# V of both mixers with tokens stationary and 512 weight columns moving, in rows of tokens

## The chip, the cores and the metric

One core of one Trainium2 chip runs the whole program. The metric is the device time of one execution in microseconds (us). The kernel before took 1684.07 us (median of 3 runs, 1683.81 to 1688.92). TensorE (PE) multiplies: a stationary operand of up to 128 columns is loaded into it (the profile's PEld rows), then a moving operand streams past it and the result lands in PSUM, in banks of 128 x 512 fp32. VectorE (DVE), ScalarE (ACT) and GpSimd (POOL) do the elementwise work, and the DMA queue of SyncE (SP) moves nearly all data, issuing in order.

## What is computed

One layer of a streaming encoder, for 1024 new tokens of a prompt and 32 tokens of a running stream that has a cache of 512: 1056 tokens, width 1024, fp32. Cut to what matters here:

```
h = rmsnorm(x, g_mix)
z = h @ w_in                       # q,k,v of mixer A (512 columns each), indexer, q,k,v of mixer B, gates
v_a = z[..., 1024:1536]            # 8 heads of 64
score = sum_h relu(q_i . k_i) * w_i ; idx = top_k(score, 256)      # which keys mixer A may see
o_a = softmax(q_a . k_a / 8 over idx) @ v_a
o_b = stick_breaking(q_b . k_b / 8) @ v_b
h2 = x + w_out(sigmoid(g_a) * (o_a @ w_ba) + sigmoid(g_b) * (o_b @ w_bb))
y = h2 + w_down(relu(w_up rmsnorm(h2))^2)
```

v_a and v_b are outputs too, with shape (tokens, 8, 64). The change touches how v_a and v_b are made, and nothing else of the mathematics.

## The kernel before

**Numbers.** Every fp32 operand x is split into a high part (`xh`, a copy rounded to the fast matmul type) and a rest (`xl`); a product takes three matmuls: high by high, rest by high, high by rest. A unit of weights is 128 x 512: a DMA into `wst`, a cast by ACT into `wh`, a subtraction on POOL into `wl`. Five places (`WB`) hold such pairs, and three buffers hold raw units. The first norm's factor per token is applied to the projection after the matmul: `rs` holds it per token in a column, `rb` spread along tokens in a row.

**Stages.** (1) index projection, to about 80 us; (2) q, k, v of mixer B for four pairs of heads, with the indexer's scores between them; (3) the top-k, a search by bits on DVE and ACT (tile `junk`, 31 bits in two groups of token tiles), then the masks; (4) two gates, and for each pair of heads of mixer A: V, then q and k (tile `qk`); (5) more gates, attention B, attention A, with gates and branch products as filler; (6) from about 915 us the merge and the feed-forward part.

**V before** (`project_v(p, mixer, w, vout)`, called at the end of `project_b` and the start of `project_a`, four times each). The weights are stationary, 128 columns of one pair of heads, and tokens move: chunks of 512, 272 and 272, eight steps of k, three matmuls each, so 72 matmuls per call, into the banks `pj` (two of them). DVE multiplies each chunk by `rb` into `vt` (head columns on partitions, tokens along), which is stored as the transposed output. The attention needs V with tokens on partitions, so PE transposes `vt` in 9 blocks of 128 into bank `t`, ACT copies the high half of each head into `vs`, DVE makes the rest, and a DMA stores `vs` to `dv`.

**What sets the order.** All work is recorded as nodes of a plan (`Plan`), and each engine's order is written out by it ahead of the run, from its own costs: among the nodes whose inputs are there, the one of the lowest rank number, then the oldest. Ranks are `FAST` (evictions), `PREP` (weights), `MAIN`, `FILL` (column-block matmuls) and `SLOW` (the top-k). On the chip each queue then runs strictly in that order and waits where the plan was wrong.

Of the kernel before, what the change touches and what calls it, by code (L numbers as in the profile page):

```python
# [10 lines left out]
F32 = mybir.dt.float32  # L11
F32R = mybir.dt.float32r
# [3 lines left out]
AF = mybir.ActivationFunctionType  # L16
# [40 lines left out]
FAST, PREP, MAIN, FILL, SLOW = 0, 1, 2, 3, 4  # L57


def rows(s):  # L60

    return DEC if s == NEW else 128
# [7 lines left out]
GROUPS = (range(0, 4), range(4, 8), range(8, 9))  # L70
# [391 lines left out]
class Layer:  # L462
# [103 lines left out]
    def run(self):  # L566
        nc, a = self.nc, self.a
# [11 lines left out]
        c = lambda shape, dt, name: nc.tile(self.const, shape, dt, name)  # L579
# [66 lines left out]
        for p in range(2, 4):  # L646
            self.project_b(p)
            with nc.behind():
                old, new = a["ck" + "ba"[p - 2]], self.dc[H * (3 - p):H * (4 - p)]
                nc.sync.dma_start(*(z.rearrange("j e t -> (j e) t") for z in (new, old)))  # L650
        with nc.rank(SLOW):
            self.top_k_begin()
        gates = iter([*range(KB, 2 * KB), *range(KB)])
        for _ in range(2):
            self.gate(next(gates), "zb")
        self.early(*(a["w_va"][0, j] for j in range(2)), *(a["w_qka"][0, j] for j in range(3)))
        nc.close(self.pr, self.ik)
        self.pr = nc.open("proja")
        self.rope_tables()
        for p in range(4):  # L660
            self.project_a(p)
        with nc.rank(SLOW):
# [390 lines left out]
                self.ts_[:, :, j].rearrange("p t (s e) -> p t s e", s=2),  # L1053
                S.rearrange("p t (s e) -> p t s e", s=2), gx)

    def project_v(self, p, mixer, w, vout):

        nc, pr = self.nc, self.pr
        units = [self.unit(w[p, j]) for j in range(2)]
        vt = nc.tile(pr, [128, T], F32, "vt", bufs=1)  # L1060

        def done(c, cs, ps):
            nc.vector.tensor_mul(vt[:, cs], ps, self.rb[:, cs])

        self.column_block(units, self.x_of, done, self.parts)
        nc.sync.dma_start(vout[p * 128:p * 128 + 128], vt)
        for sl in GROUPS:
            pt = self.bank("t")
            m = rows(sl[0])
            nt = len(sl)  # L1070
            for i, s in enumerate(sl):
                nc.tensor.transpose(pt[:m, i * 128:i * 128 + 128], vt[:, 128 * s:128 * s + m], self.ident)
            vs = nc.tile(pr, [128, 2, 4, 128], F32R, "vs", bufs=1)
            pv = pt.rearrange("p (t h e) -> p h t e", t=4, h=2)
            for h in range(2):
                vh = vs[:m, h, :nt, 0:HD]
                nc.scalar.copy(vh, pv[:m, h, :nt])
                nc.vector.tensor_sub(vs[:m, h, :nt, HD:], pv[:m, h, :nt], vh.bitcast(F32))
            for h in range(2):
                nc.sync.dma_start(self.dv[mixer * H + 2 * p + h, :m, sl[0]:sl[0] + nt], vs.bitcast(F32)[:m, h, :nt])  # L1080

    def keep(self, dst, g, cs, z):

# [4 lines left out]
    def project_b(self, p):  # L1088
        nc, pr, a = self.nc, self.pr, self.a
        for name, dst in (("w_qb", self.dq), ("w_kb", self.dk)):  # L1090
            units = [self.unit(a[name][p, j]) for j in range(2)]

            def done(c, cs, ps, name=name, dst=dst):
                n = cs.stop - cs.start
                z = nc.tile(pr, [128, 512], F32, "zb", bufs=2)[:, :n]
                zz = nc.tile(pr, [128, 2, 512], F32R, "zz", bufs=2)[:, :, :n]
                nc.vector.tensor_mul(z, ps, self.rb[:, cs])
                nc.scalar.copy(zz[:, 0], z)
                nc.gpsimd.tensor_sub(zz[:, 1], z, zz.bitcast(F32)[:, 0])
                if name == "w_kb":  # L1100
                    nc.sync.dma_start(self.o["k_b"][p * 128:p * 128 + 128, cs], z)
                self.keep(dst, H + 2 * p, cs, zz)

            self.column_block(units, self.x_of, done, self.parts)
        self.project_v(p, 1, a["w_vb"], self.o["v_b"])

    def project_a(self, p):
        nc, pr, a = self.nc, self.pr, self.a
        self.project_v(p, 0, a["w_va"], self.o["v_a"])
        units = [self.unit(a["w_qka"][p, j]) for j in range(4)]  # L1110
        qk = nc.tile(pr, [128, NT, 4, HD], F32, "qk", bufs=1)
        ss = nc.tile(pr, [128, NT, 4], F32, "ss", bufs=2)
# [2 lines left out]
        for s in range(NT):  # L1115
            m = rows(s)
# [687 lines left out]
def _host_arrays(inp):  # L1804
    f = {k: np.asarray(v) for k, v in inp.items()}

    def units(w):
        k, m = w.shape
        return np.ascontiguousarray(
            w.reshape(k // 512, 4, 128, m // 128, 128).transpose(3, 0, 2, 1, 4).reshape(m // 128, k // 512, 128, 512))  # L1810
# [10 lines left out]
        np.concatenate([qi[:, :256], ki, wi], axis=1).reshape(KB, 128, NI_A).transpose(1, 0, 2).reshape(128, KB * NI_A))  # L1821
    out["w_ib"] = np.ascontiguousarray(
        qi[:, 256:].reshape(4, 2, 128, NI_B).transpose(0, 2, 1, 3).reshape(4, 128, 512))
    out["w_qb"], out["w_kb"], out["w_vb"], out["w_va"] = units(qb), units(kb), units(vb), units(va)
# [26 lines left out]
    return out  # L1851


_OUTS = {"yT": (128, KB, T), "k_a": (T, 512), "v_a": (512, T), "k_idx": (T, HD), "k_b": (512, T), "v_b": (512, T)}


def _build(nc, arrays):
# [29 lines left out]
```

## Time and profile before

| | |
|---|---|
| median of 3 runs | 1684.07 us |
| span of the profiled execution, first to last instruction | 1682.7 us |
| what lies around the span, by the median | 1.4 us |
| PE busy / PEld busy | 1662.1 us (99%) / 1585.9 us (94%) |
| DVE / ACT / POOL busy | 1368.9 us (81%) / 947.7 us (56%) / 799.9 us (48%) |
| granted TensorE clock | 1.000 throughout |
| DMA, mean | 173 GB/s |
| first and last transposition of V | 119.5 us, 428.4 us |

The profiled execution has no time of its own beside its span here; the span with 1.4 us stands for the median run. Of a matmul the profile gives a start and a modelled end: a 272-column matmul is shown as 0.29 us long although the next one starts about 0.13 us after it. What a matmul costs a busy TensorE is therefore read from start to start, not from its length. Everything recorded through the plan has the line of the plan's own call, so groups are told apart by tile names.

### The profile page before, as it was taken

To read this page: it belongs to the slowest core of one execution; us is meant where nothing else is said; L and a number is where in the kernel's file an instruction comes from. 1 tells how busy PE (TensorE), PEld (TensorE's weight loads), DVE (VectorE), ACT (ScalarE), POOL (GpSimd) and SP (SyncE) were. 2 spreads that over 40 slices of the span, in tenths; PEclk is the share of its full clock that TensorE was granted. 3 is DMA by queue.
4 is the path that set the end of the run, shared out by engine and by line. 5 is a ranking of instruction groups with operands and counts; after the bars stand their busy time and mean duration, and the time that the engine had idled before them with its cause. 6 is when DMAs were issued, how large, how long until landed. Compare 5 with 4: busy or idle time off the path is not lost.

```text
span 1682.7 us, 34767 instructions
## 1 busy us (share of the span) xinstructions
PE 1662.1 (99%) x12226; PEld 1585.9 (94%) x12226; DVE 1368.9 (81%) x2875; ACT 947.7 (56%) x2024; POOL 799.9 (48%) x682
## 2 busy tenths in 40 slices
PE   7999999999999999999999999999999999999999
PEld 7998999999989999998999999999999999999999
DVE  8777899997569898887877649998988998679775
ACT  6556788765366767896665546333333454443431
POOL 5423332344346566354556437543433466345563
PEclk9999999999999999999999999999999999999999
DMA  7234454354583636688774643444443597676674
GB/s 260 83 103 116 139 182 144 110 150 142 161 230 97 189 88 190 173 262 256 214 204 132 186 128 127 140 151 151 151 143 135 181 327 237 203 220 210 222 227 136
DMA packets 180685, 290.29 MB, mean 173 GB/s; under 512 B 29312, under 2 KB 60512, under 8 KB 180480
## 3 DMA queue, kind: packets, MB, share of 16 engines
q1 hardware_dynamic: 180224, 287.75, 55.2%
q8 instruction: 96, 1.57, 0.4%
q14 instruction: 77, 0.63, 0.1%
q10 hardware_dynamic: 288, 0.34, 0.1%
HBM read 195.09 MB, written 94.90 MB: 172 GB/s over the span
## 4 chain that ended last, share of the span: by engine, by line
PE 87%; DVE 6%; DMA 3%; issue 2%; POOL 1%; ACT 1%; SPq 0%; DVEq 0%; ACTq 0%; POOLq 0%
PE pj L442 35%; PE c L442 11%; PE a L442 11%; PE b L442 11%; PE s L442 10%; PE o L442 5%; PE t L442 5%; DVE junk L442 2%; DMA wst<-w_ba 1%; POOL wl L442 1%; DVE y L442 0%; DMA vc<-cva 0%; DVE small L442 0%; DMA wst<-w_ib 0%; DMA xl<-du 0%
## 5 line engine op out<-in xcount | busy, mean ns | idle before, releaser
L442 PE MATMUL pj<-xl,wh 128*128 128x272 f32 (+2 forms) x1200 | 333.9, 312 | 0.0
L442 POOL TENSOR_TENSOR wl<-wst,wh 128x512 fp32r<-128x512 f32 x125 | 175.8, 1411 | 215.2 <-ACT wh L442 201.8
L442 PE MATMUL pj<-xh,wh 128*128 128x272 f32 (+1 forms) x768 | 251.8, 328 | 0.0
L442 PE MATMUL pj<-xh,wl 128*128 128x272 f32 (+1 forms) x768 | 250.6, 327 | 0.2 <-POOL wl L442 0.2
L442 PEld LDWEIGHTS pj<-xl,wh 128*128 128x128 f32 x1200 | 212.7, 188 | 9.9
L442 ACT CAST wh<-wst 128x512 fp32r<-128x512 f32 x197 | 120.5, 619 | 128.1 <-PE pj L442 34.6
L442 PEld LDWEIGHTS pj<-xh,wl 128*128 128x128 f32 x768 | 144.6, 188 | 10.6 <-POOL wl L442 0.5
L442 PEld LDWEIGHTS pj<-xh,wh 128*128 128x128 f32 x768 | 144.7, 188 | 10.2 <-DVE gz L442 0.3
L442 POOL TENSOR_TENSOR p<-p,rem 128x383 f32<-128x383 f32 (+8 forms) x66 | 104.8, 1603 | 66.4 <-DVE rem L442 29.1
L442 ACT CAST wh<-us 128x512 fp32r<-128x512 f32 x80 | 49.7, 621 | 115.9 <-PE pj L442 29.3
L442 DVE TENSOR_TENSOR tt<-t,tt 128x512 fp32r<-128x512 f32 (+2 forms) x168 | 100.2, 620 | 16.4 <-ACT tt L442 15.7
L442 DVE TENSOR_TENSOR_SCAN rem<-rem,first 128x384 f32<-128x384 f32 (+8 forms) x66 | 108.9, 1668 | 2.0 <-ACT rem L442 1.6
L442 POOL TENSOR_TENSOR wl<-y,wh 128x512 fp32r<-128x512 f32 x46 | 68.5, 1491 | 77.8 <-ACT wh L442 73.0
L442 ACT ACTIVATE junk<-score,cand 128x1024 bf16<-128x1024 f32 (+2 forms) x93 | 96.9, 1042 | 12.0 <-DVE cand L442 10.4
L442 ACT CAST wh<-y 128x512 fp32r<-128x512 f32 x79 | 48.9, 621 | 96.1 <-PE c L442 20.7
L442 ACT CAST tt<-t 128x512 fp32r<-128x512 f32 (+2 forms) x168 | 85.8, 540 | 27.3 <-PE t L442 18.3
L442 PE MATMUL o<-tt,v 128*128 128x256 f32 (+1 forms) x640 | 98.7, 279 | 1.2 <-DVE o L442 0.6
L442 PE MATMUL s<-k,q 128*128 128x512 f32 (+4 forms) x384 | 98.3, 352 | 0.6 <-issue 0.6
L442 PEld LDWEIGHTS o<-tt,v 128*128 128x128 f32 x640 | 90.5, 189 | 7.4 <-ACT tt L442 1.4
L442 DVE TENSOR_SCALAR_CACHE_REDUCE junk<-score,cand 128x384 bf16<-128x384 f32 (+1 forms) x124 | 92.9, 749 | 3.1
L442 PE MATMUL t<-ident,p 128*128 128x128 f32 (+1 forms) x596 | 90.8, 275 | 0.0
L442 POOL TENSOR_SCALAR p<-p,nb 128x384 f32<-128x384 f32 (+6 forms) x66 | 53.5, 817 | 70.6 <-DVE nb L442 57.8
(380 smaller groups left out, 5646.3 us busy)
## 6 DMA issues: line engine op xcount, KB each, us to landing
us<-w_down SPq DMA_DIRECT2D x80, 256.0 KB, 3.5
q<-dq SPq DMA_DIRECT2D x64, 256.0 KB, 4.3
du<-us SPq DMA_DIRECT2D x56, 264.0 KB, 2.7
du<-y SPq DMA_DIRECT2D x56, 264.0 KB, 3.1
y<-w_up SPq DMA_DIRECT2D x44, 256.0 KB, 2.8
k<-dk SPq DMA_DIRECT2D x40, 256.0 KB, 4.5
v<-dv SPq DMA_DIRECT2D x40, 256.0 KB, 4.2
xl<-du SPq DMA_DIRECT2D x35, 264.0 KB, 5.2
```

The costliest lines, as they stand in the source:

```text
L442: fn(*args, **kw)
```

## The change

`project_v` now makes all 512 columns of one mixer in one call. The tokens are stationary (`xh`, `xl` of one token tile) and the 512 weight columns move. Four token tiles at once fill four banks (`V_BANKS`: `pj`, `s`, `pj`, `s`), then five tiles (the last has the 32 new tokens, 64 stationary columns, two matmuls a step, and a joining addition) fill `pj`, `s`, `pj`, `s`, `s`. Each group of tiles walks the eight units of weights, so each unit is loaded twice. A finished bank is scaled by `rs` on ACT into `vz` (two buffers), which is stored as the output in rows of tokens; ACT casts the high half into `vs` (two buffers of 128 x 8 x 128) and DVE or POOL makes the rest; one DMA per tile stores all eight heads to `dv`. No transposition of V is left. V of mixer B comes after all four q and k of mixer B, V of mixer A before the first q and k of mixer A. The weights and outputs have a new layout, and the scratch that is set aside for software-driven DMA is cut to 1024.

```diff
+V_BANKS = ('pj', 's', 'pj', 's', 's')
...
+        self.project_v(1, a["w_vb"], self.o["v_b"])
         with nc.rank(SLOW):
             self.top_k_begin()
...
-        self.early(*(a["w_va"][0, j] for j in range(2)), *(a["w_qka"][0, j] for j in range(3)))
+        self.early(*(a["w_va"][k] for k in range(WB)))
...
+        self.project_v(0, a["w_va"], self.o["v_a"])
         for p in range(4):
             self.project_a(p)
...
-    def project_v(self, p, mixer, w, vout):
-        units = [self.unit(w[p, j]) for j in range(2)]
-        vt = nc.tile(pr, [128, T], F32, "vt", bufs=1)
-        def done(c, cs, ps):
-            nc.vector.tensor_mul(vt[:, cs], ps, self.rb[:, cs])
-        self.column_block(units, self.x_of, done, self.parts)
-        nc.sync.dma_start(vout[p * 128:p * 128 + 128], vt)
-        for sl in GROUPS:
-            pt = self.bank("t")
...
-                nc.tensor.transpose(pt[:m, i * 128:i * 128 + 128], vt[:, 128 * s:128 * s + m], self.ident)
-            vs = nc.tile(pr, [128, 2, 4, 128], F32R, "vs", bufs=1)
...
+    def project_v(self, mixer, w, vout):
+        mm = nc.tensor.matmul
+        for tiles in (range(0, 4), range(4, NT)):
+            banks = [self.bank(V_BANKS[i]) for i in range(len(tiles))]
+            for k in range(KB):
+                wh, wl = self.unit(w[k])
+                with nc.rank(FILL):
+                    for s, ps in zip(tiles, banks):
+                        first, last = k == 0, k == KB - 1
+                        if s == NEW:
+                            x = self.xh[1][:, k, SEQ - W1:]
+                            mm(ps[:2 * DEC], x, wh, start=first, stop=False)
+                            mm(ps[:2 * DEC], x, wl, start=False, stop=last)
+                            continue
+                        xh, xl = self.x_of(k, slice(128 * s, 128 * s + 128))
+                        mm(ps, xh, wh, start=first, stop=False)
+                        mm(ps, xh, wl, start=False, stop=False)
+                        mm(ps, xl, wh, start=False, stop=last)
+            for s, ps in zip(tiles, banks):
+                m = rows(s)
+                with nc.rank(FAST):
+                    if s == NEW:
+                        self.join(ps, nc.tile(pr, [128, 512], F32, "vz", bufs=2)[:DEC])
+                    z = nc.tile(pr, [128, 512], F32, "vz", bufs=2)
+                    nc.scalar.activation(z[:m], ps[:m], AF.Copy, scale=self.rs[:m, s:s + 1])
+                    vs = nc.tile(pr, [128, H, 128], F32R, "vs", bufs=2)
+                    zv = z.rearrange("p (h e) -> p h e", h=H)
+                    nc.scalar.copy(vs[:m, :, 0:HD], zv[:m])
+                nc.either.tensor_sub(vs[:m, :, HD:], zv[:m], vs.bitcast(F32)[:m, :, 0:HD])
+                nc.sync.dma_start(vout[128 * s:128 * s + m], z[:m])
+                nc.sync.dma_start(
+                    self.dv[mixer * H:mixer * H + H, :m, s].rearrange("g p e -> p g e"), vs.bitcast(F32)[:m])
...
-        self.project_v(p, 1, a["w_vb"], self.o["v_b"])
...
-        self.project_v(p, 0, a["w_va"], self.o["v_a"])
```

**PE, V of mixer B.** Before, in the third pair of heads (rows read "bank <- moving, stationary", and `t<-ident,vt` is a transposition):

```order
L442 MATMUL pj<-xh_106,wh_1423 128x272
L442 MATMUL pj<-xl_107,wh_1423 128x272
L442 MATMUL t<-ident,vt 128x128 x4
L442 MATMUL pj<-xh_106,wl_1424 128x272
L442 MATMUL pj<-xh_106,wh_1423 128x272
```

In the changed kernel, in the first group of four tiles (now "bank <- moving weights, stationary tokens"):

```order
L443 MATMUL pj<-wh_1437,xh_104 128x512
L443 MATMUL pj<-wl_1438,xh_104 128x512
L443 MATMUL pj<-wh_1437,xl_105 128x512
L443 MATMUL s<-wh_1437,xh_104 128x512
L443 MATMUL s<-wl_1438,xh_104 128x512
L443 MATMUL s<-wh_1437,xl_105 128x512
L443 MATMUL pj<-wh_1440,xh_104 128x512
```

The 272-column matmuls and the transpositions are gone; every matmul of V moves 512 columns, and consecutive triples go to different banks.

**PE, where the second group of V of mixer B takes over the banks of the first.** In the changed kernel, the last matmuls of the first group and the first of the second; the third waiting row is the one that needs the bank of tile 1:

```order
L443 MATMUL s<-wl_1444,xh_104 128x512
L443 MATMUL s<-wh_1443,xl_105 128x512
L443 MATMUL s<-wh_1459,xh_106 128x512 [waits Activation_49]
L443 MATMUL s<-wl_1460,xh_106 128x512 [waits Pool_49]
L443 MATMUL s<-wh_1459,xl_107 128x512
L443 MATMUL pj<-wh_1459,xh_106 128x512 [waits Activation_49]
L443 MATMUL pj<-wl_1460,xh_106 128x512
L443 MATMUL pj<-wh_1459,xl_107 128x512
L443 MATMUL s<-wh_1459,xh_106 128x512 [waits Activation_49]
```

31 rows after the first of these waits PE comes to the first matmul that needs the bank of tile 2:

```order
L443 MATMUL s<-wh_1468,xh_106 128x512
L443 MATMUL pj<-wh_1459,xh_106 128x512 [waits Activation_49]
L443 MATMUL pj<-wl_1460,xh_106 128x512
L443 MATMUL pj<-wh_1459,xl_107 128x512
L443 MATMUL s<-wh_1459,xh_106 64x512 [waits Activation_49]
```

The first unit of weights (`wh_1459`) comes up again there: tiles 4, 5 and 7 run four units ahead of tiles 6 and 8, which wait for the banks of tiles 2 and 3.

**ACT, the evictions of that first group.** In the changed kernel (`junk` are counts of the top-k, `vz` the evictions):

```order
L443 ACTIVATE vz<-pj,rs 128x512 [waits PE_49]
L443 ACTIVATE vz<-s,rs 128x512 [waits PE_49]
L443 CAST vs<-vz 128x8x64 [waits Activation_49] x2
L443 CAST wh_1471<-wst 128x512 [waits DMAHW6_49,PE_49,Pool_49]
L443 ACTIVATE junk,cntb_1500<-score_1258,cand 128x896
L443 ACTIVATE junk,cnta_1497<-score_1259,cand 128x1024 [waits DVE_49,Activation_49]
L443 ACTIVATE junk,cntb_1501<-score_1257,cand 128x768 [waits DVE_49,Activation_49]
L443 ACTIVATE vz<-pj,rs 128x512 [waits DMAHW1_49]
L443 ACTIVATE vz<-s,rs 128x512 [waits DMAHW2_49]
```

Tiles 0 and 1 are evicted together; three counts of the top-k stand between them and tiles 2 and 3, whose evictions wait for the stores of the first two `vz` buffers. Before, V's copies on ACT (`vs<-t`) stood between counts too, but PE's next chunk took its bank from a multiplication on DVE.

More of the change, by code (lines that the diff above doesn't have):

```diff
@@ L1054, in rope_tables @@
                 S.rearrange("p t (s e) -> p t s e", s=2), gx)
-    def project_v(self, p, mixer, w, vout):
+    def project_v(self, mixer, w, vout):
         nc, pr = self.nc, self.pr
-        units = [self.unit(w[p, j]) for j in range(2)]
-        vt = nc.tile(pr, [128, T], F32, "vt", bufs=1)
-        def done(c, cs, ps):
-            nc.vector.tensor_mul(vt[:, cs], ps, self.rb[:, cs])
-        self.column_block(units, self.x_of, done, self.parts)
-        nc.sync.dma_start(vout[p * 128:p * 128 + 128], vt)
-        for sl in GROUPS:
-            pt = self.bank("t")
-            m = rows(sl[0])
-            nt = len(sl)
-            for i, s in enumerate(sl):
-                nc.tensor.transpose(pt[:m, i * 128:i * 128 + 128], vt[:, 128 * s:128 * s + m], self.ident)
-            vs = nc.tile(pr, [128, 2, 4, 128], F32R, "vs", bufs=1)
[L1074 to L1080, printed above, removed]
@@ L1823, in _host_arrays @@
         qi[:, 256:].reshape(4, 2, 128, NI_B).transpose(0, 2, 1, 3).reshape(4, 128, 512))
-    out["w_qb"], out["w_kb"], out["w_vb"], out["w_va"] = units(qb), units(kb), units(vb), units(va)
+    out["w_qb"], out["w_kb"] = units(qb), units(kb)
+    out["w_vb"], out["w_va"] = (np.ascontiguousarray(z).reshape(KB, 128, 512) for z in (vb, va))
     out["w_g"] = units(np.concatenate([ga, gb], axis=1))
@@ L1851, in _host_arrays @@
     return out
-_OUTS = {"yT": (128, KB, T), "k_a": (T, 512), "v_a": (512, T), "k_idx": (T, HD), "k_b": (512, T), "v_b": (512, T)}
+_OUTS = {"yT": (128, KB, T), "k_a": (T, 512), "v_a": (T, 512), "k_idx": (T, HD), "k_b": (512, T), "v_b": (T, 512)}
 def _build(nc, arrays):
@@ L1870 @@
     arrays = _host_arrays(inputs)
-    nc = bacc.Bacc("TRN2", target_bir_lowering=False, num_devices=1)
+    nc = bacc.Bacc("TRN2", target_bir_lowering=False, num_devices=1, dynamic_dma_scratch_size=1024)
     _build(nc, arrays)
@@ L1881 @@
     kap, kas = pair(r["k_a"].reshape(T, H, HD))
-    vap, vas = pair(np.ascontiguousarray(r["v_a"].T).reshape(T, H, HD))
+    vap, vas = pair(r["v_a"].reshape(T, H, HD))
     kip, kis = pair(r["k_idx"])
     kbp, kbs = pair(np.ascontiguousarray(r["k_b"].T).reshape(T, H, HD))
-    vbp, vbs = pair(np.ascontiguousarray(r["v_b"].T).reshape(T, H, HD))
+    vbp, vbs = pair(r["v_b"].reshape(T, H, HD))
     return tuple(np.ascontiguousarray(z) for z in (yp, ys, kap, vap, kip, kbp, vbp, kas, vas, kis, kbs, vbs))
```

## The prediction

> **What bounds the kernel now.** I read the page first: the share of each engine and the chain of work that ended last.
>
> ```profile
> span 1682.7 us, 34767 instructions
> PE 1662.1 (99%) x12226; PEld 1585.9 (94%) x12226; DVE 1368.9 (81%) x2875; ACT 947.7 (56%) x2024; POOL 799.9 (48%) x682
> PEclk9999999999999999999999999999999999999999
> PE 87%; DVE 6%; DMA 3%; issue 2%; POOL 1%; ACT 1%; SPq 0%; DVEq 0%; ACTq 0%; POOLq 0%
> ```
>
> TensorE is busy from start to end at a full granted clock and carries 87% of the chain. A share of 99% could hide slack, since matmuls are shown longer than they cost, so next come the stretches that hold the work on V, by engine (PE, PEld, DVE, ACT, POOL):
>
> ```profile
> 80.00:180.00 100.00, 100.00 (x608) 89.47 (x607) 71.72 (x148) 60.31 (x133) 26.86 (x33) 1.00 0.37 106
> 180.00:260.00 80.00, 80.00 (x501) 72.49 (x501) 72.28 (x259) 71.00 (x141) 29.28 (x26) 1.00 0.58 177
> 260.00:300.00 40.00, 40.00 (x286) 37.89 (x285) 37.16 (x134) 35.53 (x67) 12.44 (x12) 1.00 0.38 131
> 300.00:345.00 45.00, 42.84 (x328) 40.33 (x328) 43.16 (x154) 33.84 (x73) 16.54 (x19) 1.00 0.41 117
> 345.00:440.00 95.00, 94.40 (x733) 90.48 (x732) 72.61 (x169) 50.06 (x112) 41.47 (x41) 1.00 0.50 149
> ```
>
> PE has no hole up to 300 us, although the top-k keeps DVE and ACT about 90% busy from 180 us on. Only in 300 to 345 us, with DVE at 43.16 of 45 us, does PE lose 2.2 us, and 0.6 us more up to 440. So what the change is worth is what it takes from TensorE's own stream, provided the engines that feed it keep up.
>
> **What one matmul and one transposition cost PE.** The timeline of PE in a stretch without a wait, start and shown length in the first two columns:
>
> ```profile
> 217.02 0.38 PE L442 MATMUL t<-ident,vt 128*128 128x128 f32 x2
> 217.16 0.37 PE L442 MATMUL pj<-xh,wh 128*128 128x272 f32 x1
> 217.37 0.29 PE L442 MATMUL pj<-xl,wh 128*128 128x272 f32 x1
> ...
> 218.37 0.39 PE L442 MATMUL pj<-xh,wh 128*128 128x512 f32 x1
> ...
> 220.00 0.49 PE L442 MATMUL t<-ident,vt 128*128 128x128 f32 x3
> 220.25 0.47 PE L442 MATMUL pj<-xl,wh 128*128 128x512 f32 x1
> 220.56 0.40 PE L442 MATMUL pj<-xh,wl 128*128 128x512 f32 x1
> ```
>
> From 217.37 to 218.37 us eight 272-column matmuls start: 0.125 us each. From 218.37 to 220.00 seven of 512 columns: 0.233 each. From 217.02 to 217.37 lie two transpositions and one 272-column matmul, so (0.35 - 0.125) / 2 = 0.112 for a transposition; from 220.00 to 220.56 three and one 512-column matmul, (0.56 - 0.233) / 3 = 0.109. I take 0.111.
>
> **The sum on PE.** Before, eight calls (four pairs, two mixers) of 24 matmuls of 512 and 48 of 272 columns, and 9 transpositions:
>
> ```profile
> L442 PE MATMUL t<-ident,vt x72: 270/272/276, 119.5 to 428.4; 128*128 128x128 f32 x64, 128*32 128x128 f32 x8
> ```
>
> 192 x 0.233 = 44.7, 384 x 0.125 = 48.0, 72 x 0.111 = 8.0: 100.7 us. After: per mixer 8 tiles x 8 steps x 3 matmuls and 16 for the new tokens, 208; for both 416 x 0.233 = 96.9 us. The gain is **3.8 us**. The new form streams more columns, 416 x 512 = 212,992 against 202,752, since the tile of 32 tokens costs as much per matmul as one of 128; what pays is the transpositions. Starts are given to 0.01 us: over seven or eight steps that is 0.0014 each, some 0.5 us on the balance of the matmuls, and 0.2 on the transpositions. So 3.1 to 4.5 us. The stationary side is now a token tile of the same 128 columns, so I keep 0.233 for it.
>
> A rule of the Trainium skill speaks against this gain. Its page "TensorE: Matmul & The Clock Gate", section "Back-to-back issue gap", gives N / 2.4 + 2.5 ns for a warm matmul of N columns, thus 215.8, 115.8 and 55.8 ns; by it V would cost 41.4 + 44.5 + 4.0 = 89.9 us before and 89.8 after, no gain. The rows above have 233, 125 and 111 ns at a granted clock of 1.00 and disagree, most for the transposition, on which it all hangs.
>
> **What moves to other engines.** Groups between 80 and 480 us, with the mean ns of one after the comma:
>
> ```profile
> L442 DVE TENSOR_TENSOR vt<-pj,rb 128x272 f32<-128x272 f32 x16 | 6.9, 433 | 4.5 <-PE pj L442 4.5
> L442 DVE TENSOR_TENSOR vt<-pj,rb 128x512 f32<-128x512 f32 x8 | 5.5, 689 | 1.5 <-PE pj L442 1.5
> L442 DVE TENSOR_TENSOR vs<-t,vs 128x256 fp32r<-128x256 f32 x32 | 12.0, 416 | 2.1 <-ACT vs L442 2.0
> L442 ACT CAST vs<-t 128x256 fp32r<-128x256 f32 x32 | 10.3, 374 | 2.2 <-PE t L442 1.0 <-DMA dv<-vs 0.9
> L442 DVE TENSOR_TENSOR az<-t,az 128x512 fp32r<-128x512 f32 x16 | 10.8, 681 | 6.6 <-ACT az L442 6.5
> L442 ACT CAST az<-t 128x512 fp32r<-128x512 f32 x16 | 9.3, 582 | 16.0 <-DMA dq<-az 15.1 <-PE t L442 0.8
> L442 ACT ACTIVATE gz<-gz 128x512 f32<-128x512 f32 x5 | 3.1, 629 | 6.3 <-DVE gz L442 6.3
> L442 ACT CAST wh<-wst 128x512 fp32r<-128x512 f32 x57 | 34.0, 615 | 11.8 <-PE pj L442 5.7 <-DMA wst<-w_kb 2.3 <-PE s L442 2.2
> L442 POOL TENSOR_TENSOR wl<-wst,wh 128x512 fp32r<-128x512 f32 x55 | 73.2, 1339 | 120.5 <-ACT wh L442 110.2 <-DMA out_k_a<-qk 9.3 <-PE s L442 0.6
> ```
>
> DVE loses 6.9 + 5.5 + 12.0 = 24.4 us and gets 14 subtractions at the price of the nearest row, 0.681: 9.5. It is relieved by 15 us, most of it in the stretch where it is short. ACT loses 10.3 and gets 18 evictions at 0.629, 18 casts at 0.582 and 16 more casts of weights at 0.615: 31.6, so 21 us more. POOL gets 16 x 1.339 = 21.4 and four subtractions, an engine that was busy 12.44 of 40 us. None of this is on PE's path as long as the top-k, which has the lowest rank, takes the delay. Were ACT its bound and the whole 21 us added to it, it would still not reach the path:
>
> ```profile
> L442 ACT ACTIVATE mask<-sq x7: 508/741/1057, 353.9 to 407.7; 128x384 bf16<-128x384 bf16 x1, 128x512 bf16<-128x512 bf16 x1, 128x640 bf16<-128x640 bf16 x1, 128x1024 bf16<-128x1024 bf16 x1
> L442 PE MATMUL s<-k,q x38: 222/342/500, 473.9 to 495.8; 128*128 128x512 f32 x16, 128*128 128x384 f32 x8, 128*128 128x256 f32 x6, 128*128 128x128 f32 x4
> ```
>
> The masks are done at 408 us, and attention B, whose tiles take their room, starts at 474: 66 us of cover, filled by gates. Without it, 21 us would be on the path.
>
> **Weights.** A unit now serves 12 or 14 matmuls, 2.8 or 3.3 us of PE, and needs 0.615 on ACT and 1.339 on POOL: less than half. SP issues 16 more loads of 256 KB, 4.2 MB at a DMA share of 0.4 to 0.6; they come ahead of need by up to five units. I price this at nothing; if ACT's counts came first each time, a unit would be late by about one count, 1.1 us, against those five units.
>
> **The turnover of banks** is the new wait. Group two starts in three free or freed banks and reaches the bank of tile 2 after 31 matmuls, 31 x 0.233 = 7.2 us after group one's end. Tile 2's eviction stands on ACT behind tile 1's, two casts, a cast of weights and three counts:
>
> ```profile
> L442 ACT ACTIVATE junk<-score,cand 128x1024 bf16<-128x1024 f32 x31 | 35.6, 1149 | 0.8 <-DVE cand L442 0.3
> L442 ACT ACTIVATE junk<-score,cand 128x896 bf16<-128x896 f32 x31 | 32.3, 1042 | 0.6
> L442 ACT ACTIVATE junk<-score,cand 128x768 bf16<-128x768 f32 x31 | 29.0, 936 | 10.6 <-DVE cand L442 10.1
> L442 ACT ACTIVATION_READ_ACCUMULATOR junk<-score,cand 128x1 f32 x93 | 17.5, 188 | 0.0
> ACT junk L442 <- DVE cand L442: 10.4, 12, 3.2
> out_v_b<-vt SPq DMA_DIRECT2D x4, 528.0 KB, 3.4
> out_v_a<-vt SPq DMA_DIRECT2D x4, 528.0 KB, 4.6
> ```
>
> Tile 1's last matmul starts 7 x 0.233 = 1.6 us before the group's end and is shown 0.4 long, so its eviction runs from -1.2 to -0.6. Casts to +0.6, weights to 1.2, counts (each with 0.188) to 2.4, 3.8 and 4.9, tile 2 evicted at **5.5 us, against 7.2**. The store that it also waits for was issued near -1.2 and lands within 4.6. So nothing is lost; one late `cand` (worst 3.2 us) would cost 3.2 - 1.7 = 1.5 us. There are two such turnovers, one per mixer: 0 to 3 us. Behind the waiting matmul every later one of PE stands, in order.
>
> **Stalls that go.** With V's DVE work out of 300 to 345 us, the 2.2 us lost there may go, though 36 tiles of q and k now follow each other with no V between: 0 to 2.8 us won or as much lost. I take zero for turnovers and stalls together, with -3 and +6 as ends.
>
> The sum against the profiled execution: 1682.7 - 3.8 = 1678.9 us of span; with the 1.4 us around it, **1680.3 us**. A measurement here can tell about 0.3%, 5 us, from no change: under 1679.0 counts as faster, over 1689.1 as slower. The forecast is a small gain just inside "no change".
>
> **Rivals.** *A, DVE's relief counts too.* For it: PE's hole lies where DVE is at 96%, and V's work on it goes. Against: the top-k refills DVE at once. Gain 3.8 + 2.2 = 6.0, perhaps a little more: 1678 us.
>
> *B, the evictions bind.* Place: the four ends of groups (one to two, and two to what follows, per mixer). All tiles of a group end within 2.6 us, two `vz` buffers make tiles 2 and 3 wait for a landing, and SP may have that store behind a load that waits for POOL. It decides once tile 2 is later than 7.2 us. Were ACT's chain of 5.5 + 1.2 us doubled by waits, tile 2 would come at 12.2: 5.0 us per mixer, 10 in all, and the matter is slower by 10 - 3.8: 1690 us. With half of that, 1685. Against: the counts waited for `cand` only 12 times in 93.
>
> *C, transpositions cost their shown length.* 72 x 0.272 = 19.6 instead of 8.0 gives 15.4 us and 1668.7. The same page of the Trainium skill, "Part 4: PE-mode transpose", has about 275 ns for one in a kernel's context, and the length agrees. Against: three of them and a matmul pass in 0.56 us.
>
> *D, a transposition is nearly hidden.* Read from 217.02 to 217.16 alone, two take 0.14 us, 0.07 each; 72 x 0.07 = 5.0 leaves 0.8 us, 1683.3. Against: the matmul behind them is 0.21 before the next instead of 0.125, and that pause comes with them. The rule of the issue gap above would end here too.
>
> **How the numbers follow.** Forecast 0.43, A 0.32, B 0.13, C 0.03, D 0.09. Faster by over 0.3%: most of A, all of C and a tenth of the forecast, 0.39. Slower: half of B, 0.08. Within: 0.53. The range takes the forecast's ends, -3 and +6 around 1680.3 with the sum's own half microsecond, and is drawn to 1674 and 1687: below lies C, above the worse half of B.
>
> **What would show it.** After: no `t<-ident,vt`; V's matmuls 0.233 apart; 232 fewer matmuls and transpositions in all; PE without a hole where the second groups start, or, for B, a wait of PE on ACT `vz` there and ACT `vz` waiting for `out_v`; for A, a fuller PE in the stretch of the first q and k; the masks done well before attention B starts. I am wrong if a 512-column matmul with tokens stationary is not 0.233 us, or if the later stages, whose order shifts with the plan, gain or lose more than 3 us.

## The result, and the profile after

The changed kernel takes 1697.29 us (median of 4 runs, 1695.45 to 1697.48) against 1684.42 us for the kernel before on the same chip: ratio 1.0071, 95% interval 1.0059 to 1.0084. It is 0.7% slower, where 1680.3 us and a range of 1674 to 1687 were forecast. The first lines of its page:

```profile
span 1695.7 us, 34240 instructions
PE 1666.7 (98%) x11994; PEld 1579.8 (93%) x11994; DVE 1364.6 (80%) x2819; ACT 963.5 (57%) x2028; POOL 826.4 (49%) x702
PE   8999999988999999999999999999999999999999
PEclk9999999998999999999999999999999999999999
```

There are 232 PE instructions fewer, as the sum had it, yet the span is 13.0 us longer. The rows of digits cut the span into 40 slices of 42 us. In PE's row the first slice is short in the kernel before too; the ninth and tenth (339 to 424 us) fall below 9 only here. The granted clock falls below 9 in the tenth alone. The windows show more. The engines by stage (PE, PEld, DVE, ACT, POOL, then the granted clock), in the changed kernel:

```profile
180.00:260.00 80.00, 80.00 (x403) 66.83 (x402) 64.84 (x221) 74.02 (x138) 38.65 (x33) 1.00 0.68 206
260.00:320.00 60.00, 60.00 (x298) 49.88 (x297) 52.77 (x177) 56.11 (x105) 31.27 (x27) 1.00 0.59 182
320.00:345.00 25.00, 25.00 (x199) 24.19 (x198) 20.04 (x64) 21.04 (x40) 5.65 (x6) 1.00 0.55 166
345.00:440.00 95.00, 84.51 (x641) 81.48 (x640) 78.02 (x186) 52.77 (x107) 37.05 (x39) 0.91 0.41 109
440.00:480.00 40.00, 38.05 (x242) 34.57 (x241) 20.53 (x47) 12.43 (x28) 14.97 (x16) 0.96 0.49 136
```

V is made in the first two rows (mixer B at 204 to 252 us, mixer A at 275 to 323), and there PE has no hole. The whole loss stands in 345 to 480 us: q and k of mixer A, which now follow one another with no V between. In 345 to 440 us PE was busy 94.40 of 95 us before; now 84.51, at a mean granted clock of 0.91.

A landmark dates the loss. Up to the first matmul of attention B (`s<-k,q`) both kernels do the same work, V apart. It started at 473.9 us before; in the changed kernel:

```profile
L443 PE MATMUL s<-k,q x72: 220/342/499, 486.8 to 551.4; 128*128 128x512 f32 x30, 128*128 128x384 f32 x12, 128*128 128x256 f32 x12, 128*128 128x320 f32 x12
```

486.8 - 473.9 = 12.9 us of the 13.0 are lost by then, and nothing behind it. If V itself is 3.8 us shorter, the stretch of q and k costs 12.9 + 3.8 = 16.7 us more.

**V is what the prediction said.** PE's timeline over the end of the first group of tiles and the beginning of the second, V of mixer B:

```profile
224.29 0.39 PE L443 MATMUL s<-wh,xh 128*128 128x512 f32 x1
...
226.12 0.39 PE L443 MATMUL s<-wh,xl 128*128 128x512 f32 x1
226.35 0.40 PE L443 MATMUL s<-wh,xh 128*128 128x512 f32 x1
...
235.91 0.39 PE L443 MATMUL pj<-wh,xh 128*128 128x512 f32 x1
```

Fifty starts lie between 224.29 and 235.91: 0.232 us each (forecast 0.233), straight through the turnover of the banks at 226.35.

**What is late between pairs.** POOL's waits between 290 and 480 us in the changed kernel (engine, line, what waits, for whom: us in total, times, longest):

```profile
POOL qk L443 <- DMA out_k_a<-qk: 15.6, 2, 7.8
POOL qk L443 <- PE t L443: 8.7, 1, 8.7
```

And in the kernel before, the same stretch:

```profile
POOL qk L442 <- PE t L442: 10.4, 2, 9.6
POOL wl L442 <- DMA out_k_a<-qk: 9.3, 1, 9.3
```

PE's longest wait in that stretch of the changed kernel is for `az`, the copies of the transposed q and k:

```profile
PE t L443 <- DVE az L443: 4.3, 3, 2.2
```

Tile `qk` has one buffer. It holds q and k of one pair, all nine token tiles, until DVE has normalised k, PE has transposed q and k (into the banks `t`, from which ACT and DVE make `az`) and the store `out_k_a` has read it; only then may POOL clear its last part and write it for the next pair. So POOL, in order, sits for 8 to 10 us: three times in the changed kernel, and in the kernel before, twice. What differs is what PE has to do meanwhile. The rows of one such turnover in the changed kernel (start, length; timeline, by engine SP, DVE, POOL, PE; `SPq` rows are issues on SP's DMA queue):

```profile
366.35 1.69 SPq L443 DMA_DIRECT2D out_k_a<-qk  x3
...
364.73 1.35 DVE L443 TENSOR_TENSOR qk<-qk,f 128x1152 f32<-128x1152 f32 x1
372.07 1.49 DVE L443 TENSOR_TENSOR_SCAN pre<-sq,minus 128x640 f32<-128x640 bf16 x1 [1.36 <-ACT sq L443]
373.79 0.42 DVE L443 TENSOR_TENSOR tb<-pj,tabs 128x256 f32<-128x256 f32 x1
...
370.08 0.31 POOL L443 MEMSET qk<- 128x256 f32 x1 [7.73 <-DMA out_k_a<-qk]
...
369.17 0.28 PE L443 MATMUL s<-wh,xl 128*128 128x256 f32 x1
369.41 0.24 PE L443 MATMUL t<-ident,qk 32*128 32x32 f32 x1
371.14 0.33 PE L443 MATMUL t<-ident,qk 128*128 128x128 f32 x1 [1.49 <-POOL qk L443]
374.35 0.55 PE L443 MATMUL pj<-wh,xh 128*128 128x256 f32 x1 [2.88 <-DVE needa L443]
374.70 0.42 PE L443 MATMUL pj<-wl,xh 128*128 128x256 f32 x1
...
379.18 0.28 PE L443 MATMUL pj<-wl,xh 128*128 128x256 f32 x1
```

Read it upwards from 374.35. PE waits for a bank `pj`, which is free once DVE has made `ta` and `tb` from it (`tb` at 373.79). The row names `needa`, a small operation of DVE right behind `tb`, which PE does not read. Each of `ta` and `tb` has one buffer too, and POOL, which adds the tile before into `qk`, was held until 370.08 by the store issued at 366.35; that needed k normalised at 364.73. Between POOL and `tb` DVE also ran a scan of the top-k (372.07), after an idle 1.36 us for ACT. In the meantime PE had filled its five banks: 24 matmuls at 0.118 us each, 2.8 us a bank, some 14 us in all. After 369.17 it did only two transpositions in 5 us. At the other two turnovers PE stops at its own transpositions of `qk`, whose bank is free only once DVE has made `az` from it (2.2 us up to 410.50, 1.6 us up to 442.14), and POOL waits behind them. Before, V of the next pair stood here: 24 x 0.233 + 48 x 0.125 = 11.6 us that need no `qk`.

The hole has a price beyond its length. The granted clock around it:

```profile
370.00:374.00 4.00, 0.33 (x1) 0.14 (x1) 2.64 (x5) 2.19 (x5) 1.00 (x2) 0.79 0.78 214
376.00:378.00 2.00, 2.00 (x11) 2.00 (x11) 1.14 (x4) 2.00 (x4) 0.74 (x1) 0.50 0.10 16
380.00:382.00 2.00, 2.00 (x20) 2.00 (x19) 1.44 (x2) 0.95 (x2) 0.00 (x0) 1.00 0.00 0
```

At 376 to 378 us the clock is 0.50 and eleven matmuls start where at 380 to 382 twenty do. From 374.70 to 379.18 lie 21 steps, 0.213 us each instead of 0.118: 2.0 us lost after PE had its work back. Three more such stretches follow, at 390.6 to 392.9, 411.5 to 416.4 and 444.1 to 447.1 us; all four hold 71 steps of 256 columns at about 0.213 us, some 6.7 us too much; the kernel before has no such stretch there. So of the 16.7 us about 6.7 are slow matmuls, and only the rest is waiting. The Trainium skill, "TensorE: Matmul & The Clock Gate", "Part 1: The HAM clock gate", says that the clock falls to half after an idle window of about 3.4 us and rises after a busy one of that length; these rows agree in kind (half speed behind some 5 us that were nearly idle), with 4.6 us at half speed here. The stretch at 390.6 does not fit: between 384.3 and 390.2 us PE's four waits are 0.95, 0.26, 0.17 and 0.44 us long, no idle window of 3.4, and yet the clock reads 0.50 at 390 to 392 us. What set it off is open.

### The profile page after: what moved, and what is told of

Its sections match the earlier page's. It is cut to its first block, busy times and chain, and to the rows that moved or that the text cites. A ratio compares the mean times of both kernels' runs of the same rounds, so it can differ in the third digit from the quotient of the medians.

```text
span 1695.7 us, 34240 instructions
## 1 busy us (share of the span) xinstructions
PE 1666.7 (98%) x11994; PEld 1579.8 (93%) x11994; DVE 1364.6 (80%) x2819; ACT 963.5 (57%) x2028; POOL 826.4 (49%) x702
## 5 line engine op out<-in xcount | busy, mean ns | idle before, releaser
L443 PE MATMUL pj<-xl,wh 128*128 128x272 f32 (+2 forms) x1008 | 273.1, 310 | 0.0
L443 PE MATMUL pj<-xh,wh 128*128 128x272 f32 (+1 forms) x576 | 188.6, 327 | 0.0
L443 PE MATMUL pj<-xh,wl 128*128 128x272 f32 (+1 forms) x576 | 188.0, 326 | 0.0
L443 PEld LDWEIGHTS pj<-xl,wh 128*128 128x128 f32 x1008 | 176.7, 188 | 7.4
L443 POOL TENSOR_TENSOR p<-p,rem 128x383 f32<-128x383 f32 (+7 forms) x66 | 103.6, 1584 | 65.4 <-DVE rem L443 25.6
L443 PEld LDWEIGHTS pj<-xh,wh 128*128 128x128 f32 x576 | 108.4, 188 | 7.7
L443 PEld LDWEIGHTS pj<-xh,wl 128*128 128x128 f32 x576 | 108.5, 188 | 7.3
L443 DVE TENSOR_TENSOR_SCAN rem<-rem,first 128x384 f32<-128x384 f32 (+7 forms) x66 | 105.6, 1620 | 3.7 <-ACT rem L443 3.3
L443 PE MATMUL s<-wh,xh 128*128 128x256 f32 (+3 forms) x344 | 106.1, 314 | 1.6 <-DVE f L443 0.6
L443 PE MATMUL s<-wl,xh 128*128 128x256 f32 (+3 forms) x344 | 105.6, 312 | 0.0
```

What stands on the lines that cost most here:

```text
L443: fn(*args, **kw)
```

## The experiments

The theory: **the turnover of `qk` was always there, and V's matmuls between the pairs covered it; V moved ahead leaves it bare.** Rivals: the new form of V itself disturbs what follows (its weights, its evictions); or DVE's top-k is the cause, with `qk` only named. The landmark in the table is the first matmul of attention B, in the profiled run. The runs come from several chips, each with runs of the kernel before beside it, so kernels are best compared by their ratios.

| kernel | median, us | ratio to before (95%) | landmark, us |
|---|---|---|---|
| before | 1684.42 | 1 | 473.9 |
| changed | 1697.29 | 1.0071 (1.0059, 1.0084) | 486.8 |
| before's form, V of A moved ahead | 1706.99 | 1.0137 (1.0122, 1.0153) | 497.9 |
| new form for B only | 1680.39 | 0.9977 (0.9966, 0.9987) | 468.5 |
| changed, two `qk` | 1687.01 | 1.0021 (1.0012, 1.0029) | 476.2 |
| before, two `qk` | 1685.26 | 1.0006 (0.9997, 1.0015) | 473.7 |
| changed, top-k cut | 1689.46 | 1.0029 (1.0018, 1.0040) | 479.2 |
| before, top-k cut | 1681.52 | 0.9991 (0.9981, 1.0001) | 471.3 |
| changed, two `qk`, top-k cut | 1678.48 | 0.9965 (0.9953, 0.9978) | 468.1 |
| changed, V of A only between pairs | 1700.82 | 1.0103 (1.0088, 1.0117) | 489.8 |
| changed, a gate after each of three pairs | 1705.69 | 1.0133 (1.0120, 1.0147) | 496.9 |
| changed, two `qk`, a gate after two pairs | 1697.17 | 1.0080 (1.0067, 1.0094) | 486.7 |
| changed, two `qk`, V of A in 4, 3, 2 tiles | 1688.96 | 1.0026 (1.0017, 1.0036) | 476.8 |
| new form for B only, two `qk` | 1684.11 | 1.0002 (0.9993, 1.0011) | 472.2 |

### Only the place: the old form of V, moved ahead

```diff
-        self.early(*(a["w_va"][0, j] for j in range(2)), *(a["w_qka"][0, j] for j in range(3)))
+        self.early(*(a["w_va"][p, j] for p, j in ((0, 0), (0, 1), (1, 0), (1, 1), (2, 0))))
...
         self.rope_tables()
+        for p in range(4):
+            self.project_v(p, 0, a["w_va"], self.o["v_a"])
         for p in range(4):
             self.project_a(p)
...
-        self.project_v(p, 0, a["w_va"], self.o["v_a"])
```

> The kernel before with the four calls of V of mixer A, in their old form with transpositions, moved together ahead of the first q and k. Turnover theory: the placement alone makes the stall, 1684 + 17 = about 1700 us, ratio 1.008 to 1.012, with the clock below 1 between 350 and 460 us. Form theory (the new form, its layouts or its ordering of queues makes the loss): no slower than the kernel before, ratio 0.998 to 1.002.

Not one matmul differs from the kernel before, only the place of V of mixer A and which weights are loaded early, and it is 1.37% slower, more than the 0.8 to 1.2% expected. Its windows:

```profile
300.00:340.00 40.00, 34.62 (x224) 31.34 (x223) 36.51 (x129) 31.72 (x66) 5.14 (x4) 0.94 0.27 96
380.00:420.00 40.00, 33.98 (x252) 32.29 (x251) 28.00 (x61) 16.51 (x34) 11.93 (x15) 0.91 0.47 122
```

PE loses 6.0 us between pairs in the second row, with a clock of 0.91, much as in the changed kernel, and POOL waits 9.9, 9.1 and 8.7 us ahead of its three clearings of `qk`. So the place is enough. (The first row is V itself: its transpositions wait once 3.7 us for DVE, which is at the top-k.) The rival "the new form disturbs" is not needed for the loss.

### Only the form: the new V for mixer B alone

```diff
-        self.early(*(a["w_va"][k] for k in range(WB)))
+        self.early(*(a["w_va"][0, j] for j in range(2)), *(a["w_qka"][0, j] for j in range(3)))
...
-        self.project_v(0, a["w_va"], self.o["v_a"])
         for p in range(4):
+            self.project_v_old(p, 0, a["w_va"], self.o["v_a"])
             self.project_a(p)
...
```

This is against the changed kernel; `project_v_old` is the V of the kernel before, at its old place and with its old layout of weights and output.

> New form and place for V of mixer B alone; V of mixer A stays in its old form, in front of each pair of q and k. Turnover theory: no new stall, and half the gain on PE's stream, 1.9 to 2.1 us: 1682 us, ratio 0.9988. Form theory: part of the loss shows with B too, ratio 1.003 or more.

1680.39 us, faster than both kernels. Its windows in the stretch of q and k of A, where V stands between again:

```profile
340.00:380.00 40.00, 40.00 (x313) 38.53 (x312) 36.43 (x107) 26.56 (x62) 16.44 (x18) 1.00 0.55 155
380.00:420.00 40.00, 40.00 (x313) 38.40 (x312) 33.90 (x71) 23.90 (x47) 17.46 (x16) 1.00 0.52 144
```

No hole. The gain, 0.0023 x 1684.4 = 3.9 us (2.2 to 5.7), is above the 1.9 us that half of the sum gives. PE's loss of 1.7 us in the kernel before at 320 to 345 us is gone too, and 1.9 + 1.7 would be near 3.9; why the changed order of B does that was not tried apart.

### Two buffers of qk

```diff
-        qk = nc.tile(pr, [128, NT, 4, HD], F32, "qk", bufs=1)
+        qk = nc.tile(pr, [128, NT, 4, HD], F32, "qk", bufs=2)
```

In the changed kernel:

> The changed kernel with two buffers for the tile qk in place of one, nothing else. Turnover theory: the first writes of the next pair no longer wait for the transpositions and stores of the last; POOL's waits for out_k_a (15.6 us) and for PE's transpositions (8.7 us) go, and with them most of the stall: 1680 to 1684 us, ratio 0.998 to 1.000. DVE theory: DVE has the same work in the same stretch, so the stall stays, 1692 to 1697, ratio 1.005 to 1.008.

1687.01 us: 10.3 us of the 12.9 come back by this one number (8.4 of 12.0 by the ratios). That lies between the two forecasts, 1680 to 1684 and 1692 to 1697, nearer to the first. In the kernel before:

> The kernel before with two buffers of qk. If V's matmuls covered the turnover of qk, as the theory says, the second buffer is worth at most the 2.8 us that PE lost there in 300 to 440 us: 1681.5 to 1684.5. Rival: a second buffer is worth some 10 us in any order (it won 10.3 in the changed kernel), 1674.

No gain: 1.0006 (0.9997 to 1.0015), so the rival, some 10 us in any order, falls. But the run does not take POOL's wait away: POOL uses the second buffer to clear for one pair further ahead, at the same places in its queue (339.96 and 378.24 us), and still sits 9.8 us before the second of them. That the wait costs nothing in the kernel before is therefore read from that kernel itself: PE is busy 39.68 of 40 us at 340 to 380 and 39.79 at 380 to 420, where POOL's two long waits lie. What still stops PE in the changed kernel with two buffers, from its timeline (DVE and PE):

```profile
382.48 2.57 DVE L443 TENSOR_TENSOR_SCAN pre<-sq,minus 128x1024 f32<-128x1024 bf16 x1 [0.41 <-ACT sq L443]
...
386.09 1.27 DVE L443 SCALAR_TENSOR_TENSOR pre<-pre,needa,sgn 128x1024 f32<-128x1024 f32 x1
387.28 0.41 DVE L443 TENSOR_TENSOR ta<-pj,tabc 128x256 f32<-128x256 f32 x1
387.62 0.41 DVE L443 TENSOR_TENSOR tb<-pj,tabs 128x256 f32<-128x256 f32 x1
...
388.17 0.36 PE L443 MATMUL pj<-wh,xh 128*128 128x256 f32 x1 [2.77 <-DVE rw L443]
```

PE again waits for a bank whose `ta` and `tb` are made late, this time behind the scan and the comparison with which the top-k makes its masks. That suggested the next pair.

### The top-k cut, with one buffer and with two

```diff
-        for b in range(30, -1, -1):
+        for b in range(30, 28, -1):
...
-        for g in self.groups:
-            ...                        # thresholds, last counts, scans and masks of each group
+        for t in range(2, 8):
+            nc.gpsimd.memset(self.mask[t], 0.0)
+        nc.gpsimd.memset(self.mask[8][0:32], 0.0)
```

The changed kernel, the kernel before, and the changed kernel with two buffers:

> The changed kernel without most of the top-k: two bits in place of 31, and the masks set to zero in place of the end of the top-k, so every earlier key is let through. What it leaves out is 93% of the counts and the whole end. DVE theory: with DVE and ACT free the stall in the stretch of q and k is gone; against the kernel before with the same left out it is faster by about 4 us. Turnover theory: the way from the last tile of one pair to the first write of the next (norm, transpositions, store) is shorter, but still there: at least half of the stall stays, and it is slower than the kernel before with the same left out by 4 us or more.

> The kernel before without most of the top-k (two bits of 31, masks set to zero): the reference for the run without top-k of the changed kernel. PE bounds the kernel, so it is faster than the kernel before only by the stalls that the top-k made, 2 to 5 us: 1680 us. Both theories expect the same here.

> The changed kernel with two buffers of qk and, as in the earlier pair without it, most of the top-k left out (2 of 31 bits, masks zero), so that its output is not the reference's. What is left of the loss in the kernel with two buffers (its PE is busy 16.27 of 20 us at 380 to 400, behind DVE's scans of the masks) is DVE's top-k tail, says the theory: then nothing is left here, and the time is that of the changed kernel without top-k less the whole stall, 1679 to 1682 us, no gap over 1 us between pairs. Rival, the other single or double buffers of a turnover (az, ta, tb) and their stores hold the rest: 1684 us or more, with gaps of 2 us or more at the turnovers.

Windows of the changed kernel without the top-k, one buffer of `qk`:

```profile
340.00:380.00 40.00, 35.53 (x277) 34.16 (x276) 21.58 (x57) 12.83 (x29) 14.69 (x19) 0.96 0.45 120
380.00:420.00 40.00, 37.75 (x306) 37.20 (x305) 25.12 (x60) 13.12 (x31) 18.39 (x22) 0.96 0.45 122
```

With two buffers:

```profile
340.00:380.00 40.00, 37.49 (x310) 36.32 (x309) 22.87 (x62) 15.53 (x35) 17.16 (x21) 1.00 0.44 120
380.00:420.00 40.00, 40.00 (x338) 39.47 (x337) 29.70 (x72) 11.65 (x30) 18.41 (x23) 1.00 0.53 139
```

With DVE busy little more than half the time the holes are still there with one buffer: POOL waits for PE's transpositions in three turnovers,

```profile
POOL qk L443 <- PE t L443: 26.7, 3, 9.3
```

and with two buffers that row falls to

```profile
POOL qk L443 <- PE t L443: 2.6, 2, 2.3
```

So "DVE alone" falls as well. The medians split the loss. Without the top-k, the changed kernel is 1689.46 - 1681.52 = 7.9 us slower than before; two buffers take back 11.0, and what is left is 3.0 us faster than before (4.4 by the two ratios, 0.9965 against 0.9991): near the forecast gain of the new form. Put back, the top-k costs 2.9 us in the kernel before (1.5 by the ratio, which does not exclude nothing), 7.8 in the changed one and 8.5 in the one with two buffers: some 5 to 6 us more where V no longer stands between (5.6 and 7.9 by the ratios). Together: -3.0 + 11.0 + 4.9 = 12.9. This sum closes by the way it is made; it splits the difference and is no further proof of it.

The time of 1678.48 us is just below what was expected; the 2.5 us that PE still loses at 340 to 380 was not expected.

### Something else between the pairs

V itself, in three groups of three tiles, one behind each of the first three pairs:

```diff
-        self.early(*(a["w_va"][k] for k in range(WB)))
+        self.early(*(a["w_qka"][0, j] for j in range(4)))
...
-        self.project_v(0, a["w_va"], self.o["v_a"])
         for p in range(4):
             self.project_a(p)
+            if p < 3:
+                self.project_v(0, a["w_va"], self.o["v_a"], (range(3 * p, 3 * p + 3),))
```

> The changed kernel, with V of mixer A cut into three groups of three token tiles that are recorded after the first, second and third pair of q and k (weights loaded three times, 24 units in place of 16). Turnover theory: PE stalls because the one buffer of the tile qk has to be normalised, transposed and stored before the next pair of q and k can be written, and V's matmuls were what PE did in that time. With V back between the pairs the 24 us that PE lost between 340 and 460 us fall to about 6 as before, and the clock stays at 1.00: 1697 - 17 = 1680 us, a ratio to the kernel before of about 0.998. DVE theory (q and k evictions and the end of the top-k together ask more of DVE than it has): V between spreads that too, 1680 to 1686. If the stall were in the new form of V itself (its banks, its stores), it would stay: 1697.

A miss: 1700.82 us, far from 1680 to 1686 and nearest to the 1697 of a stall in V's new form. The waits say otherwise. The largest one of its PE, and POOL at that time:

```profile
PE s L443 <- DVE small L443: 7.6, 1, 7.6
```

```profile
286.64 1.42 POOL L443 TENSOR_TENSOR tabc<-ropec,gqk 128x576 f32<-128x576 f32 x1
...
290.76 1.39 POOL L443 TENSOR_TENSOR tabs<-ropes,gqk 128x576 f32<-128x576 f32 x1
```

The first pair now comes earlier, and POOL is still making the rope tables that `ta` and `tb` read, until 292.15 us; DVE's counts of the top-k then hold `ta` to 294.07 and `tb` to 295.70, and PE goes on at 296.26. V ahead of the pairs had covered that, and taking it away opened a hole of 7.6 us; a later turnover lost some 5 us more where DVE's normalisation of `qk` took 6.10 us instead of 1.35. V's own evictions (PE on ACT `vz`) held PE for 2.5 us.

Gates, three of those that stood behind the last pair and ahead of attention B:

```diff
-GATES_BEFORE, GATES_FIRST = 4, 3
+GATES_BEFORE, GATES_FIRST = 5, 2
         for p in range(4):
             self.project_a(p)
+            if p < 3:
+                self.gate(next(gates))
...
-        for _ in range(GATES_BEFORE - 2):
-            self.gate(next(gates))
```

> The changed kernel with one gate (72 matmuls, 11.6 us of PE) after each of the first three pairs of q and k; the gates are taken from behind the fourth pair and from the first filler of attention, so the work is the same. Turnover theory: any filler of PE will do, so the stall goes as with V between: 1680 us, ratio about 0.998, unless attention misses the gate that it gave up as filler (up to 3 us). DVE theory: a gate asks only 1.6 us of DVE in 11.6 us, so this helps too, 1680 to 1686.

A miss: 1705.69 us, 8.4 above the changed kernel. The windows, between the pairs and behind the last one:

```profile
420.00:460.00 40.00, 40.00 (x312) 38.52 (x312) 20.56 (x51) 14.46 (x29) 14.57 (x17) 1.00 0.40 108
460.00:480.00 20.00, 8.86 (x57) 7.29 (x56) 11.34 (x31) 6.09 (x13) 6.96 (x8) 0.72 0.23 60
```

Between the pairs PE is full, with one buffer of `qk`: the matmuls of a gate, which need no `qk`, cover as those of V do. But the last pair has a turnover too, its transpositions and stores ahead of attention B, and the gates taken from there leave 11.1 of 20 us empty, with a clock of 0.72.

The best of both, as it seemed: two buffers, two gates between, one behind.

```diff
-GATES_BEFORE, GATES_FIRST = 4, 3
+GATES_BEFORE, GATES_FIRST = 5, 2
...
             self.project_a(p)
+            if p in (0, 1):
+                self.gate(next(gates))
...
-        for _ in range(GATES_BEFORE - 2):
-            self.gate(next(gates))
+        self.gate(next(gates))
...
-        qk = nc.tile(pr, [128, NT, 4, HD], F32, "qk", bufs=1)
+        qk = nc.tile(pr, [128, NT, 4, HD], F32, "qk", bufs=2)
```

> The changed kernel with two buffers of qk, and three gates (one taken from ahead of attention B) of which one each is recorded behind the first and the second pair and one behind the last. Theory: a turnover needs other matmuls of PE beside it or a second buffer, and with both nothing is lost between pairs, while the one gate behind the last pair keeps its end covered: 1677 to 1681 us, the whole gain of the new form in both mixers. Rival: the missing gate behind the last pair opens the hole there that the kernel with one gate after each pair had (14.9 us at 460 to 480): 1686 or more.

The rival holds: 1697.17 us. Its windows behind the last pair:

```profile
460.00:480.00 20.00, 15.95 (x93) 13.98 (x92) 8.41 (x18) 4.04 (x11) 2.26 (x3) 0.91 0.52 137
480.00:500.00 20.00, 17.39 (x110) 15.35 (x108) 11.16 (x18) 11.76 (x28) 7.58 (x6) 1.00 0.97 278
```

Three gates behind the last pair instead of five do not cover its own turnover (PE waits 3.8 us for `az`) and the loads of attention B (2.6 us for `q`). The gates are one stock: those set between the pairs are missing at the end.

V of mixer A split, so that none of the gates is needed:

```diff
-        self.project_v(0, a["w_va"], self.o["v_a"])
+        self.project_v(0, a["w_va"], self.o["v_a"], (range(4),))
         for p in range(4):
             self.project_a(p)
+            if p < 2:
+                self.project_v(0, a["w_va"], self.o["v_a"], (range(4, 7), range(7, NT))[p:p + 1])
...
-        qk = nc.tile(pr, [128, NT, 4, HD], F32, "qk", bufs=1)
+        qk = nc.tile(pr, [128, NT, 4, HD], F32, "qk", bufs=2)
```

> The changed kernel with two buffers of qk, and V of mixer A in three groups of 4, 3 and 2 token tiles: the first stays ahead of q and k (over the building of the rope tables, which held the first q and k in the run with V only between), the second is recorded behind the first pair, the third behind the second. What two buffers alone left was lost at the first two turnovers (340 to 420 us), and there V's 512-column matmuls stand now. Theory: the loss of 300 to 480 us falls back to that of the kernel before, and the time is 1678 to 1682 us. Rival: a group of V between pairs waits for its own banks and evictions, as it did in the run with V only between (PE on ACT vz 2.1 us, PE on ACT sq 2.7 us at 340 to 360), and the turnovers stay open: 1686 us or more.

1688.96 us, no better than two buffers alone, and in the range of the rival. A wait of its PE in 355 to 400 us:

```profile
PE pj L443 <- POOL wl L443: 2.2, 3, 1.0
```

A group of two or three tiles uses a unit of weights for 5 or 9 matmuls, 1.2 or 2.1 us, and POOL needs about 1.3 us for its half beside the additions into `qk`. With such small groups PE waits for weights, 2.2 us on POOL and 1.4 on ACT; with the groups of four and five tiles of the change it does not. PE is idle 6.7 us at 345 to 440, so these are about half of it; the rest was not followed.

### The second buffer in the fastest kernel

The new form for B only, with `bufs=2` for `qk`.

> V of mixer B in the new form, V of mixer A in the old one and in its old place, and two buffers of qk. The stretch of q and k lost at most 0.9 us per 20 us with one buffer, so a second one has little to win: 1678 to 1681, against 1680.4 with one. Rival: the new order that two buffers give moves V away from the turnovers it covers, 1683 or more.

A miss: 1684.11 us, 3.7 us above the same kernel with one buffer. One row of its PE:

```profile
350.43 0.55 PE L443 MATMUL t<-ident,vt 128*128 128x128 f32 x3 [1.07 <-DVE vt L443]
```

With the buffer free earlier the plan writes another order, and now V's own transpositions wait for `vt` behind DVE's counts; PE is busy 37.43 of 40 us in 340 to 380. With one buffer it was full there, so 2.6 of the 3.7 us are lost in this stretch, 1.1 of them in the row shown; the rest was not followed.

## Why the prediction was wrong, point by point

- **The sum on PE, -3.8 us: right.** 0.232 us a matmul, 232 instructions fewer, and 3.0 to 4.4 us faster where the turnovers no longer bind (two buffers, top-k cut). The rule of the Trainium skill ("TensorE: Matmul & The Clock Gate", "Back-to-back issue gap") that left no gain, and that this section gives for an isolated matmul, does not fit these figures. Nor does D (0.8 us) or C (15.4): with the intervals of both ratios the gain is about 1.7 to 7.1 us, which does not tell 3.0 from 4.4 or from A's 6.0.
- **Rival A, DVE's relief: seen, and far too small.** PE is full at 320 to 345 us, where it lost 1.7 us before; V of mixer A ends at 323 us, and q and k of the first pair run there without a hole, with DVE busy 20.04 of 25 us. The turnovers behind it lose far more than this wins.
- **Weights, evictions, the turnover of banks, priced at 0 to 3 us: right at zero.** PE has no hole in 180 to 320 us. Rival B named the ends of V's groups; nothing waits there.
- **Other engines off the path: half right.** DVE was relieved, but the top-k is not only the one that takes the delay. Its scans and comparisons stand in DVE's queue ahead of `ta` and `tb`, and with no V between they cost some 5 to 6 us more. "66 us of cover" was measured to attention B, the wrong reader: the sooner one is the bank that PE needs next.
- **"Stalls that go ... though 36 tiles of q and k now follow each other with no V between: 0 to 2.8 us won or as much lost. I take zero" is the step that failed.** It measured 16.7 us lost. The bound was taken from what PE lost there before, which was small because V covered the wait: 11.6 us of V per pair against 9.3 to 9.6 us of POOL waiting for `qk`. The row that says so was quoted in the prediction, for its other half: POOL `wl` with `<-DMA out_k_a<-qk 9.3` near its end. The step that would have found it is to ask, for each piece of work that moves, which wait it had covered at its old place. The two rows of POOL's waits before, 10.4 + 9.3 = 19.7 us, were a better guess at the loss to be had from that profile than 2.8. That 16.7 lies near it is partly luck: about 6.7 of it are matmuls at half clock, which no row before shows, and POOL's waits for `qk` grew to 15.6 + 8.7 = 24.3.
- **A slip in the chances:** half of B's 0.13 is 0.065 and not the 0.08 that stands for "slower"; nothing hangs on it.
- **The clause on what would make it wrong** named later stages that shift with the plan. They did not: the landmark holds all of the loss but 0.1 us.

No kernel with the new form in both mixers that does the whole work was found to beat the kernel before. The fastest that does it is the new form in mixer B alone, 1680.39 us; there, moving V laid no wait bare (PE is busy 80.00 of 80 us at 180 to 260).

## What to carry to other kernels

Work that looks like load on the busiest engine can be the cover of somebody's wait: before moving it, look on every other in-order engine for waits of about its length at its old place (here POOL, 9.3 to 9.6 us against 11.6 us of matmuls), and price them as bare. Cover is a stock that can be spent once, so moving filler from one turnover to another moves the hole with it. A hole on TensorE is to be priced with the slow clock behind it.

## What the runs showed that was not expected

- Behind about 5 us that were nearly idle the matmuls of 256 columns follow at 0.213 us instead of 0.118 for 4.6 us; this was 2.0 us on top of the hole, and with the three stretches that follow 6.7 us of the whole loss.
- DVE's normalisation `qk<-qk,f` takes 1.34 to 1.36 us in 52 of the 56 cases of all fourteen profiles, about 2.46 us in three and 6.10 us in one, in the kernel with V only between. There POOL was busy with subtractions, most of them for `wl`, nearly all of that time, as these rows of DVE and POOL show:

```profile
422.85 6.10 DVE L443 TENSOR_TENSOR qk<-qk,f 128x1152 f32<-128x1152 f32 x1 [0.63 <-POOL qk L443]
...
422.79 1.27 POOL L443 TENSOR_TENSOR vs<-vz,vs 128x512 fp32r<-128x512 f32 x1
424.03 3.71 POOL L443 TENSOR_TENSOR wl<-wst,wh 128x512 fp32r<-128x512 f32 x3
```

  POOL's run ends at 427.74 and DVE's operation at 428.95, 1.2 us later, about its usual length. The other cases agree. In the three of 2.45 to 2.48 us (B only; V in 4, 3, 2 tiles; changed with the top-k cut) a POOL subtraction of 1.28 to 1.29 us had begun 0.02 to 0.04 us ahead of DVE's operation, which again ends 1.2 us after POOL's. Where DVE's began first, POOL's subtraction is the long one: in the changed kernel 2.26 us from 463.70, against DVE's 463.45 to 464.81. A `MEMSET` of POOL beside DVE's operation (two gates, at 464.98 us) lengthened neither. So in all these cases the two operations ran one after the other; what keeps them apart was not tried.
- In the profile of the changed kernel with two buffers the granted clock reads 0.95 in nearly every window (over the whole span 0.948, against 0.998 to 1.000 in the other runs of that kernel), also where matmuls follow at the usual 0.118 us. What that figure means there stays open; nothing above rests on it.
